# Delta-rule blocks: the convolution's tail three hook steps later, the decay matrices in a chain of their own, one head ahead

## The chip, the cores and the metric

The kernel runs on one core of a Trainium2 chip, as one program of some 40,000 instructions. The metric is the device time of one execution in microseconds (us); lower is better. A core has these engines, each with a queue that it works off in order: PE (TensorE, matmuls and transposes; its weight loads are shown as PEld), DVE (VectorE), ACT (ScalarE), POOL (GpSimd) and SP (SyncE, which here issues every DMA). They meet through semaphores only.

## The reference, cut to what matters

One decoder layer: RMS norm, one wide input projection, two token mixers (a gated delta rule, "DN", and dilated window attention), gates, an output projection, a residual. The change touches the DN inputs. Per head (four heads of width 128, sequence 2048, chunks of 64):

```python
h = rms_norm(x, norm_w); proj = h @ w_in
qkv = silu(causal_depthwise_conv(dn_qkv, conv_w))       # width 4
dq, dk = l2_normalize(dq) * HEAD_DIM ** -0.5, l2_normalize(dk)
gc    = cumsum(g)                                       # log decay, per head and position
decay = exp(where(causal, gc[:, None] - gc[None, :], -inf))
lower   = where(strict, (k * beta) @ k.T * decay, 0)    # inverted later: I + lower
a_intra = where(causal, q @ k.T * decay, 0)
```

## The kernel before

All matmul inputs are float32 split in two float32r parts, so a dense product is three matmuls. The normalised input lies on chip as `hh` and `hl`, in four blocks of 512 positions. The program has stages; the one that matters is `cunits`, which makes 128 projected channels at a time:

- A *unit* is 128 channels; it has four *blocks* (`n` = 0 to 3), one for each 512 positions. A block is 24 dense matmuls (L400 to L402) into a PSUM tile `mm` (three buffers), with one call of `hook()` after every six: four *hook steps* a block. Then the unit's function is called with the block's PSUM tile.
- The units in order: three `z` units, then for each head a k unit, a q unit and a v unit (`k_block`, `q_block`, `v_block`), then the other `z` units and sixteen `g` units. Under the later ones run the inverse of the 64x64 triangles (DVE) and the scan over chunks.
- `self.at(d, fn)` puts `fn` on a list; it is called d hook steps later. So hooks set the order in which instructions are *written down*. The order in each engine's queue is made after that, when the program is built, by a list scheduler with a plan of its own: of the instructions whose inputs and buffers are ready in its plan it takes the one written down first. An instruction written late can so stand early in a queue.

What the three block functions do:

- `conv` (all three): ACT copies the PSUM tile to `xr` (L500) and makes a first product `acc` (L503); DVE adds three shifted products (L505); ACT takes a tanh (L507) and DVE ends the SiLU (L508) into `kT` or `qT`.
- `k_block`: `kT` goes to DRAM (`recput`, L511). A DMA fetches the cumulated log decay, spread over all partitions, to `gcb` (L523, one buffer); DVE adds the mask (L526) and combines (L530, four); ACT takes four exponentials (L532) into the decay matrix `E`. `E` is one tile of 16 matrices, for a whole head. Eight and nine hook steps later, `pe(0)` and `pe(2)` transpose two 128x128 parts of `kT` each (L539) to a PSUM tile `tp` (two buffers), which ACT reads (L543, L544), and POOL makes norms in seven small steps (L552 to L558).
- `q_block`: k and q are split again for the products of k with k and q: ACT copies (`kqh`, L574 and L576), POOL subtracts for k (L575) and DVE for q (L577) into `kql`. `kqh`, `kql` and `la` have one buffer. `pe(0)` and `pe(2)`, again 8 and 9 hook steps later, do for each of two parts one transpose (L585) and three matmuls into the PSUM tile `sc` (L586 to L588, where L587 needs both halves of `kql`); ACT squares the transposed parts (L590), DVE multiplies by `E` into `la` (L591); after the second one `la` goes out by four DMAs and POOL makes norms in three steps (L603 to L605).
- `v_block`: four transposes (L618), 8 hook steps after the block, and ACT scales them (L621).

Of the kernel before, what the change touches and what calls it, by code (L numbers as in the profile page):

```python
# [6 lines left out]
F32 = mybir.dt.float32  # L7
# [34 lines left out]
class Net:  # L42
# [449 lines left out]
    def conv(self, n, ct, pr, dst):  # L492
        nc, dp = self.nc, self.dp
        xr = dp.tile([P, 515], F32, name="xr", bufs=2)
        if n == 0:
            nc.gpsimd.memset(xr[:, 0:3], 0.0)
        else:
            nc.vector.tensor_copy(xr[:, 0:3], self.xr[:, 512:515])
        self.xr = xr
        nc.scalar.activation(xr[:, 3:515], pr, AF.Copy)  # L500
        acc = dp.tile([P, 512], F32, name="acc", bufs=2)
        w = self.cw[:, ct, :]
        nc.scalar.activation(acc, pr, AF.Identity, scale=w[:, 3:4])  # L503
        for j in (2, 1, 0):
            nc.vector.scalar_tensor_tensor(out=acc, in0=xr[:, j:j + 512], scalar=w[:, j:j + 1], in1=acc,  # L505
                                           op0=ALU.mult, op1=ALU.add)
        nc.scalar.activation(dst, acc, AF.Tanh, scale=0.5)  # L507
        nc.vector.scalar_tensor_tensor(out=dst, in0=dst, scalar=1.0, in1=acc, op0=ALU.add, op1=ALU.mult)  # L508
# [4 lines left out]

    def k_block(self, h, n, pr):
        nc, dp = self.nc, self.dp
        if n == 0:
            self.kT = dp.tile([P, T], F32, name="kT", bufs=1)
            self.E = dp.tile([P, 16, P], F32, name="E", bufs=1)
        kT, E = self.kT[:, n * 512:(n + 1) * 512], self.E
        self.conv(n, 4 + h, pr, kT)  # L520
        self.recput(n, h, R_KT, P, kT.rearrange("p (a c) -> p a c", c=P))
        gcb = dp.tile([P, 2, 4, P], F32, name="gcb", bufs=1)
        nc.sync.dma_start(gcb.rearrange("p a b c -> p a (b c)"),  # L523
                          dr(self.gcscr, h * T + n * 512, [[0, P], [H * T, 2], [1, 512]]))
        En = E[:, n * 4:n * 4 + 4, :]
        nc.vector.tensor_tensor(out=gcb[:, 1], in0=gcb[:, 1], in1=self.cmask.unsqueeze(1).to_broadcast([P, 4, P]),  # L526
                                op=ALU.add)
        for t in range(4):
            c = h * 16 + n * 4 + t
            nc.vector.scalar_tensor_tensor(out=gcb[:, 0, t], in0=gcb[:, 0, t], scalar=self.ngc[:, c:c + 1],  # L530
                                           in1=gcb[:, 1, t], op0=ALU.add, op1=ALU.add)
            nc.scalar.activation(En[:, t, :], gcb[:, 0, t], AF.Exp, bias=self.nlc[:, c:c + 1])  # L532
        ss = dp.tile([P, 12], F32, name="ss", bufs=2)
        kd = dp.tile([P, 4, P], F32, name="st4", bufs=2)

# [23 lines left out]
        self.at(8, lambda: pe(0))  # L559
        self.at(9, lambda: pe(2))  # L560

    def q_block(self, h, n, pr):
        nc, dp = self.nc, self.dp
        qT = dp.tile([P, 512], F32, name="qT", bufs=2)
        self.conv(n, h, pr, qT)
        self.recput(n, h, R_QT, P, qT.rearrange("p (a c) -> p a c", c=P))
        kT, E = self.kT, self.E
# [6 lines left out]
        nc.scalar.activation(kqh[:, :, 0, :], kv, AF.Copy)  # L574
        nc.gpsimd.tensor_tensor(out=kql[:, :, 0, :], in0=kv, in1=kqh[:, :, 0, :].bitcast(F32), op=ALU.subtract)  # L575
        nc.scalar.activation(kqh[:, :, 1, :], qv, AF.Copy)  # L576
        nc.vector.tensor_tensor(out=kql[:, :, 1, :], in0=qv, in1=kqh[:, :, 1, :].bitcast(F32), op=ALU.subtract)  # L577

        def pe(t0):
            pt = self.ps.tile([P, 512], F32, name="tp", bufs=2)  # L580
            pk = self.ps.tile([P, 512], F32, name="sc", bufs=2)
            for t in (t0, t0 + 1):
                b = pk[:, (t - t0) * 256:(t - t0) * 256 + 256]
                rh, rl = (a[:, t].rearrange("p a c -> p (a c)") for a in (kqh, kql))
                nc.tensor.transpose(pt[:, (t - t0) * P:(t - t0 + 1) * P], qT[:, t * P:(t + 1) * P], self.ident)  # L585
                nc.tensor.matmul(b, kqh[:, t, 0, :], rh, start=True, stop=False)  # L586
                nc.tensor.matmul(b, kqh[:, t, 0, :], rl, start=False, stop=False)  # L587
                nc.tensor.matmul(b, kql[:, t, 0, :], rh, start=False, stop=True)  # L588
            for t in (t0, t0 + 1):
                nc.scalar.activation(sq, pt[:, (t - t0) * P:(t - t0 + 1) * P], AF.Square, accum_out=ss[:, t:t + 1])  # L590
            nc.vector.tensor_tensor(out=la[:, t0:t0 + 2], in0=pk.rearrange("p (a b c) -> p a b c", b=2, c=P),  # L591
                                    in1=E[:, n * 4 + t0:n * 4 + t0 + 2, :].unsqueeze(2).to_broadcast([P, 2, 2, P]),
# [13 lines left out]
        self.at(8, lambda: pe(0))  # L606
        self.at(9, lambda: pe(2))

    def v_block(self, h, n, pr):
        nc, dp = self.nc, self.dp  # L610
        vT = dp.tile([P, 512], F32, name="qT", bufs=2)
        self.conv(n, 8 + h, pr, vT)
# [10 lines left out]
        self.at(8, pe)  # L623
# [280 lines left out]
    def run(self):  # L904
# [69 lines left out]
        self.cunits(first + du + rest, {3: open_dn, 15: lambda: self.at(9, start_inverse)}, tail)  # L974
# [61 lines left out]
```

## Time and profile before

| | |
|---|---|
| time, three runs | 2415.37, 2414.56, 2415.00 us; median 2415.0 us |
| span of the profiled execution | 2415.5 us (first to last instruction, the only time that it has of its own; 0.5 us over the median) |
| busy: PE, PEld, DVE, ACT, POOL | 2360.4, 2144.5, 1165.6, 848.5, 825.0 us |
| mean granted clock of PE | 0.996 |
| k, q and v units of the four heads | 1126.9 to 1463.5 us of the span |
| a unit with nothing else on PE (z4, from 1486.6 us) | 21.98 us |
| k, q and v unit of head 1 | 25.47, 30.05 and 28.57 us |

A line of the profile gives the source line, the engine, the operation, the tiles (out<-in), the busy time and the mean duration of one, and what the engine waited for before it. PE's busy time counts a matmul to its modelled end, so 98% is no proof of full speed; how close matmuls start behind one another tells more. The clock column is the share of full TensorE speed that was granted. What an engine waited for is inferred from semaphores.

### The profile page before, as it was taken

The page shows a single profiled execution, that of the slowest core. Times are in us where ns is not written, and L with a number is a line of the kernel's source. Part 1 is how long each engine was busy: PE and PEld are TensorE (multiplying, and loading weights), DVE is VectorE, ACT ScalarE, POOL GpSimd, SP SyncE. Part 2 cuts the span into 40 slices and gives each one's busy share as a digit, 9 for nine tenths or more (in the row PEclk, how much of TensorE's full clock was granted, in tenths as well). Part 3 has the DMA queues.
Part 4 walks back from the last instruction along what each step waited for, and adds up shares of the span by engine and source line. Part 5 has one row for each costly group of instructions (what it writes and reads, how often), then busy time and mean ns, then how long its engine had stood idle before and what let it go on. Part 6 is the DMA issues. An engine that isn't in the chain of part 4 may idle for free.

```text
span 2415.5 us, 40131 instructions
## 1 busy us (share of the span) xinstructions
PE 2360.4 (98%) x13710; PEld 2144.5 (89%) x13710; DVE 1165.6 (48%) x2738; ACT 848.5 (35%) x2985; POOL 825.0 (34%) x1785
## 2 busy tenths in 40 slices
PE   7999999999999999999999999999999999999999
PEld 7999999999999999987777778888888878889998
DVE  5644333233343433344766665999444433454431
ACT  5644433334443333323665663111243313111110
POOL 4433334433333334411433451111133212433441
PEclk9999999999999999999999999999999999999999
DMA  5211102333433343433544443222566655555442
GB/s 157 73 48 39 28 25 64 94 92 102 114 106 92 112 118 89 115 98 102 129 120 111 116 119 113 75 75 73 180 198 195 185 162 158 162 180 161 146 139 76
DMA packets 348819, 274.22 MB, mean 114 GB/s; under 512 B 57864, under 2 KB 317256, under 8 KB 348232
## 3 DMA queue, kind: packets, MB, share of 16 engines
q1 hardware_dynamic: 348616, 271.66, 39.1%
q8 instruction: 109, 1.79, 0.3%
q14 instruction: 94, 0.77, 0.1%
HBM read 167.47 MB, written 104.10 MB: 112 GB/s over the span
## 4 chain that ended last, share of the span: by engine, by line
PE 83%; DMA 7%; DVE 3%; ACT 3%; issue 2%; POOL 2%; SPq 1%; ACTq 0%; DVEq 0%; POOLq 0%
PE mm L167 10%; PE mm L169 10%; PE mm L168 10%; PE mm L400 8%; PE mm L402 8%; PE mm L401 8%; DMA gcb<-gcscr 3%; PE mm L888 2%; PE mm L886 2%; PE mm L887 2%; PE mm L869 2%; PE mm L871 2%; PE mm L870 2%; PE po L265 2%; PE tp L222 2%
## 5 line engine op out<-in xcount | busy, mean ns | idle before, releaser
L167 PE MATMUL mm<-wh,hh 128*128 128x384 f32 (+1 forms) x1536 | 553.5, 360 | 3.8 <-ACT wh L79 3.8
L169 PE MATMUL mm<-wh,hl 128*128 128x384 f32 (+1 forms) x1536 | 519.3, 338 | 0.0
L168 PE MATMUL mm<-wl,hh 128*128 128x384 f32 (+1 forms) x1536 | 518.6, 338 | 0.1
L400 PE MATMUL mm<-hh,wh 128*128 128x512 f32 x1152 | 467.2, 406 | 0.0
L402 PE MATMUL mm<-hh,wl 128*128 128x512 f32 x1152 | 454.9, 395 | 0.0
L401 PE MATMUL mm<-hl,wh 128*128 128x512 f32 x1152 | 453.5, 394 | 0.0
L167 PEld LDWEIGHTS mm<-wh,hh 128*128 128x128 f32 x1536 | 289.9, 189 | 6.6 <-ACT wh L79 4.2
L168 PEld LDWEIGHTS mm<-wl,hh 128*128 128x128 f32 x1536 | 290.7, 189 | 0.4 <-POOL wl L80 0.4
L169 PEld LDWEIGHTS mm<-wh,hl 128*128 128x128 f32 x1536 | 289.2, 188 | 0.0
L402 PEld LDWEIGHTS mm<-hh,wl 128*128 128x128 f32 x1152 | 217.6, 189 | 47.6
L400 PEld LDWEIGHTS mm<-hh,wh 128*128 128x128 f32 x1152 | 218.1, 189 | 44.5
L401 PEld LDWEIGHTS mm<-hl,wh 128*128 128x128 f32 x1152 | 218.2, 189 | 41.2
L80 POOL TENSOR_TENSOR wl<-raw,wh 128x512 fp32r<-128x512 f32 (+1 forms) x75 | 108.1, 1453 | 397.6 <-ACT wh L79 397.5
L190 DVE SCALAR_TENSOR_TENSOR rec<-mm,st,wqk 128x128 f32<-128x128 f32 x256 | 78.1, 347 | 264.1 <-POOL st L188 233.6
L186 POOL TENSOR_SCALAR st<-st 128x2 f32<-128x2 f32 x192 | 44.9, 234 | 419.8 <-ACT rec L182 284.5
L249 ACT ACTIVATE p<-sc,ol 128x128 f32<-128x128 f32 (+1 forms) x192 | 82.1, 427 | 299.3 <-DVE ol L247 287.3
L869 PE MATMUL mm<-oh,hh 128*128 128x256 f32 x512 | 143.8, 281 | 1.9 <-DVE gt L873 1.9
L505 DVE SCALAR_TENSOR_TENSOR acc<-xr,cw,acc 128x512 f32<-128x512 f32 x144 | 122.6, 851 | 44.1 <-ACT acc L503 40.7
L871 PE MATMUL mm<-oh,hl 128*128 128x256 f32 x512 | 142.9, 279 | 0.0
L870 PE MATMUL mm<-ol,hh 128*128 128x256 f32 x512 | 142.9, 279 | 0.0
L188 POOL TENSOR_TENSOR st<-st,mhalf 128x2 f32<-128x2 f32 x192 | 135.1, 704 | 16.0
L79 ACT ACTIVATE wh<-raw 128x512 fp32r<-128x512 f32 (+1 forms) x145 | 90.0, 632 | 110.8 <-PE mm L401 73.4
(240 smaller groups left out, 4320.4 us busy)
## 6 DMA issues: line engine op xcount, KB each, us to landing
raw<-in_w_in_dram SPq DMA_DIRECT2D x144, 256.0 KB, 3.3
rscr<-rec SPq DMA_DIRECT2D x128, 192.0 KB, 1.9
qk<-rscr SPq DMA_DIRECT2D x128, 128.0 KB, 2.3
gscr<-gt SPq DMA_DIRECT2D x64, 256.0 KB, 2.5
gt<-gscr SPq DMA_DIRECT2D x64, 256.0 KB, 3.5
oscr<-ol SPq DMA_DIRECT2D x192, 65.0 KB, 1.9
oc<-oscr SPq DMA_DIRECT2D x16, 780.0 KB, 5.0
rec<-rec SPq DMA_DIRECT2D x16, 768.0 KB, 5.6
```

Of the source, the lines that this page charges most:

```text
L80: eng.tensor_tensor(out=l, in0=raw, in1=h.bitcast(F32), op=ALU.subtract)
L167: nc.tensor.matmul(pr[:, :w], a, wh[:, k, :w], start=(k == 0), stop=False)
L168: nc.tensor.matmul(pr[:, :w], a, wl[:, k, :w], start=False, stop=False)
L169: nc.tensor.matmul(pr[:, :w], b, wh[:, k, :w], start=False, stop=(k == KT - 1))
L188: nc.gpsimd.tensor_tensor(out=st[:, 2:4], in0=st[:, 0:2], in1=self.mhalf[:, 0:2], op=ALU.pow)
L400: nc.tensor.matmul(pr, wh[:, k, :], a, start=(k == 0), stop=False)
L401: nc.tensor.matmul(pr, wh[:, k, :], b, start=False, stop=False)
L402: nc.tensor.matmul(pr, wl[:, k, :], a, start=False, stop=(k == KT - 1))
L505: nc.vector.scalar_tensor_tensor(out=acc, in0=xr[:, j:j + 512], scalar=w[:, j:j + 1], in1=acc, op0=ALU.mult, op1=ALU.add)
L869: nc.tensor.matmul(o, self.wbh[:, k, ms], oh[:, k, :], start=(k == b * 4), stop=False)
L870: nc.tensor.matmul(o, self.wbh[:, k, ms], ol[:, k, :], start=False, stop=False)
L871: nc.tensor.matmul(o, self.wbl[:, k, ms], oh[:, k, :], start=False, stop=(k == b * 4 + 3))
```

## The change

- `conv` writes down its last two steps (tanh L507 and the SiLU's end L508), and all that follows on them, three hook steps later, in a function `gate`. The transposes then come six and seven hook steps after that: 9 and 10 after the block in k and q, 8 as before in v.
- The decay matrices leave `k_block`. A function `e_chain` fetches `gcb`, adds the mask on POOL (not DVE) four hook steps later, and combines and exponentiates one step after that. `E` is now a tile for each block, with four buffers. The chain of head 0 is started when the DN memory is opened, a block every 6 hook steps; that of head h+1 after the first v block of head h, a block every 8 hook steps, so it is spread over the v unit of one head and the k unit of the next.
- In `q_block` both subtractions into `kql` are on POOL (the one for q was on DVE), and `pe` writes its two transposes ahead of its six matmuls instead of one ahead of each three.
- The inverse starts 12 hook steps into the unit behind the last v unit, not 9.
- Some comments are gone.

```diff
-    def conv(self, n, ct, pr, dst):
+    def conv(self, n, ct, pr, dst, then):
...
-        nc.scalar.activation(dst, acc, AF.Tanh, scale=0.5)
-        nc.vector.scalar_tensor_tensor(out=dst, in0=dst, scalar=1.0, in1=acc, op0=ALU.add, op1=ALU.mult)
+        def gate():
+            nc.scalar.activation(dst, acc, AF.Tanh, scale=0.5)
+            nc.vector.scalar_tensor_tensor(out=dst, in0=dst, scalar=1.0, in1=acc, op0=ALU.add, op1=ALU.mult)
+            then()
+        self.at(3, gate)
...
+    def e_chain(self, h, period, n=0):
+        if h == H:
+            return
+        nc, dp = self.nc, self.dp
+        gcb = dp.tile([P, 2, 4, P], F32, name="gcb", bufs=1)
+        nc.sync.dma_start(gcb.rearrange("p a b c -> p a (b c)"),
+                          dr(self.gcscr, h * T + n * 512, [[0, P], [H * T, 2], [1, 512]]))
+        def low():
+            nc.gpsimd.tensor_tensor(out=gcb[:, 1], in0=gcb[:, 1],
+                                    in1=self.cmask.unsqueeze(1).to_broadcast([P, 4, P]), op=ALU.add)
+        def high():
+            E = self.E[h, n] = dp.tile([P, 4, P], F32, name="E", bufs=4)
+            for t in range(4):
+                c = h * 16 + n * 4 + t
+                nc.vector.scalar_tensor_tensor(out=gcb[:, 0, t], in0=gcb[:, 0, t], scalar=self.ngc[:, c:c + 1],
+                                               in1=gcb[:, 1, t], op0=ALU.add, op1=ALU.add)
+            for t in range(4):
+                c = h * 16 + n * 4 + t
+                nc.scalar.activation(E[:, t, :], gcb[:, 0, t], AF.Exp, bias=self.nlc[:, c:c + 1])
+        self.at(4, low)
+        self.at(5, high)
+        if n + 1 < NB:
+            self.at(period, lambda: self.e_chain(h, period, n + 1))
...
     def k_block(self, h, n, pr):
...
-            self.E = dp.tile([P, 16, P], F32, name="E", bufs=1)
...
+        def then():
+            self.recput(n, h, R_KT, P, kT.rearrange("p (a c) -> p a c", c=P))
+            self.at(6, lambda: pe(0))
+            self.at(7, lambda: pe(2))
...
-        self.at(8, lambda: pe(0))
-        self.at(9, lambda: pe(2))
+        self.conv(n, 4 + h, pr, kT, then)
...
     def q_block(self, h, n, pr):
...
-        nc.scalar.activation(kqh[:, :, 0, :], kv, AF.Copy)
-        nc.gpsimd.tensor_tensor(out=kql[:, :, 0, :], in0=kv, in1=kqh[:, :, 0, :].bitcast(F32), op=ALU.subtract)
-        nc.scalar.activation(kqh[:, :, 1, :], qv, AF.Copy)
-        nc.vector.tensor_tensor(out=kql[:, :, 1, :], in0=qv, in1=kqh[:, :, 1, :].bitcast(F32), op=ALU.subtract)
+        def then():
+            self.recput(n, h, R_QT, P, qT.rearrange("p (a c) -> p a c", c=P))
+            for j, src in enumerate((kv, qv)):
+                nc.scalar.activation(kqh[:, :, j, :], src, AF.Copy)
+                nc.gpsimd.tensor_tensor(out=kql[:, :, j, :], in0=src, in1=kqh[:, :, j, :].bitcast(F32),
+                                        op=ALU.subtract)
+            self.at(6, lambda: pe(0))
+            self.at(7, lambda: pe(2))
...
             for t in (t0, t0 + 1):
+                nc.tensor.transpose(pt[:, (t - t0) * P:(t - t0 + 1) * P], qT[:, t * P:(t + 1) * P], self.ident)
+            for t in (t0, t0 + 1):
...
-                nc.tensor.transpose(pt[:, (t - t0) * P:(t - t0 + 1) * P], qT[:, t * P:(t + 1) * P], self.ident)
...
     def v_block(self, h, n, pr):
...
-        self.at(8, pe)
+        self.conv(n, 8 + h, pr, vT, lambda: self.at(5, pe))
+        if n == 0:
+            self.e_chain(h + 1, 8)
...
             self.dp = pool(dst, "dp", "right")
+            self.E = {}
+            self.e_chain(0, 6)
...
-        self.cunits(first + du + rest, {3: open_dn, 15: lambda: self.at(9, start_inverse)}, tail)
+        self.cunits(first + du + rest, {3: open_dn, 15: lambda: self.at(12, start_inverse)}, tail)
```

More of the change, by code (lines that the diff above doesn't have):

```diff
@@ L517, in k_block @@
             self.kT = dp.tile([P, T], F32, name="kT", bufs=1)
-            self.E = dp.tile([P, 16, P], F32, name="E", bufs=1)
[L519 to L532, printed above, removed]
+        kT = self.kT[:, n * 512:(n + 1) * 512]
         ss = dp.tile([P, 12], F32, name="ss", bufs=2)
         kd = dp.tile([P, 4, P], F32, name="st4", bufs=2)
+        def then():
+            self.recput(n, h, R_KT, P, kT.rearrange("p (a c) -> p a c", c=P))
+            self.at(6, lambda: pe(0))
+            self.at(7, lambda: pe(2))
         def pe(t0):
@@ L564, in q_block @@
         qT = dp.tile([P, 512], F32, name="qT", bufs=2)
-        self.conv(n, h, pr, qT)
-        self.recput(n, h, R_QT, P, qT.rearrange("p (a c) -> p a c", c=P))
-        kT, E = self.kT, self.E
+        kT = self.kT
         ss = dp.tile([P, 12], F32, name="ss", bufs=2)
@@ L605, in pe @@
                 G.tensor_scalar(out=self.cq[:, cs], in0=ss[:, 4:8], scalar1=SCALE, scalar2=None, op0=ALU.mult)
-        self.at(8, lambda: pe(0))
-        self.at(9, lambda: pe(2))
+        self.conv(n, h, pr, qT, then)
     def v_block(self, h, n, pr):
@@ L611, in v_block @@
         vT = dp.tile([P, 512], F32, name="qT", bufs=2)
-        self.conv(n, 8 + h, pr, vT)
         vs = dp.tile([P, 4, P], F32, name="st4", bufs=2)
```

2 lines of the change are left out of this document (1 added, 1 removed).

## The prediction, as it was put on record before the changed kernel had run

> **What bounds the kernel now.** I read the page first, then the busy times of the DN units, then PE's waits there, then the order of time around the longest.
>
> ```profile
> PE 2360.4 (98%) x13710; PEld 2144.5 (89%) x13710; DVE 1165.6 (48%) x2738; ACT 848.5 (35%) x2985; POOL 825.0 (34%) x1785
> PE 83%; DMA 7%; DVE 3%; ACT 3%; issue 2%; POOL 2%; SPq 1%; ACTq 0%; DVEq 0%; POOLq 0%
> ```
>
> PE carries the kernel, and the change removes no PE work, so all it can win is time in which PE stands still. The windows of head 1's k, q and v units, of head 2's q unit and of a bare unit (us, then busy time of PE, PEld, DVE, ACT, POOL, granted clock, DMA), and of single blocks, give how much that is:
>
> ```profile
> 1213.97:1239.44 25.47, 23.82 (x114) 19.26 (x112) 15.96 (x30) 15.30 (x45) 4.23 (x3) 1.00 0.48 114
> 1239.44:1269.49 30.05, 27.89 (x132) 22.72 (x132) 19.14 (x32) 20.36 (x71) 19.84 (x37) 0.94 0.47 126
> 1269.49:1298.06 28.57, 28.06 (x147) 23.32 (x145) 18.98 (x28) 15.65 (x49) 10.69 (x14) 1.00 0.50 108
> 1323.83:1353.85 30.02, 27.88 (x133) 22.68 (x133) 19.56 (x32) 20.36 (x71) 19.81 (x37) 0.94 0.47 127
> ...
> 1262.09:1269.49 7.40, 7.40 (x42) 6.30 (x41) 4.80 (x8) 4.33 (x14) 4.78 (x10) 1.00 0.45 119
> 1298.06:1304.00 5.94, 5.94 (x31) 4.90 (x30) 4.17 (x8) 4.41 (x12) 2.88 (x2) 1.00 0.30 78
> 1486.56:1492.05 5.49, 5.49 (x25) 4.51 (x24) 2.29 (x2) 1.61 (x3) 2.58 (x2) 1.00 0.67 217
> ```
>
> A bare block takes 5.49 us, one with four transposes 5.94, one with a q block's sixteen extra PE instructions 7.40. A head without stalls is then 12 x 5.49 + 8 x 0.45 + 4 x 1.91 = 77.1 us; head 1 takes 25.47 + 30.05 + 28.57 = 84.1. So some 7 us a head, under 30 us in all, could be won. PE's own waits (waited for, us, times, longest), over all DN units and then without those of head 0's k and q, and DVE's largest DMA wait, say where:
>
> ```profile
> PE tp L539 <- ACT st L544: 11.9, 7, 2.2
> ...
> PE tp L539 <- ACT st L544: 9.8, 5, 2.2
> PE sc L587 <- DVE kql L577: 1.6, 4, 0.5
> PE sc L587 <- POOL kql L575: 0.6, 1, 0.6
> ...
> DVE gcb L526 <- DMA gcb<-gcscr: 25.1, 16, 3.4
> ```
>
> The k transposes wait for ACT to empty `tp`. Why ACT is late is in the order of time (start, us, engine, line, idle before and its releaser):
>
> ```profile
> 1241.99 0.69 DVE L508 SCALAR_TENSOR_TENSOR kT<-kT,acc 128x512 f32<-128x512 f32 x1 [0.70 <-ACT kT L507]
> 1246.08 1.21 DVE L526 TENSOR_TENSOR gcb<-gcb,cmask 128x512 f32<-128x512 f32 x1 [3.40 <-DMA gcb<-gcscr]
> 1250.48 0.63 ACT L507 ACTIVATE kT<-acc 128x512 f32<-128x512 f32 x1 [4.21 <-DVE acc L505]
> 1253.53 0.66 PE L539 MATMUL tp<-ident,kT 128*128 128x128 f32 x2 [2.16 <-ACT st L544]
> 1254.41 0.63 PE L401 MATMUL mm<-hl,wh 128*128 128x512 f32 x1
> ```
>
> DVE stands 3.40 us before the mask for a DMA that has not landed; the convolution behind it in DVE's queue is late, so ACT stands 4.21 us before the tanh, so `tp` is emptied late, so PE stands 2.16 us, and then a dense matmul takes 0.63 us. That q unit has a granted clock of 0.94, as has head 2's. The chain is thus: DMA of `gcb`, DVE, ACT, PE, clock. Who wrote this load so early is the next view, of SP and ACT:
>
> ```profile
> 1168.97 0.36 SPq L523 DMA_DIRECT2D gcb<-gcscr  x1
> 1240.57 0.36 SPq L523 DMA_DIRECT2D gcb<-gcscr  x1
> 1288.88 1.28 ACT L532 ACTIVATE E<-gcb,nlc 128x128 f32<-128x128 f32 x4
> 1291.28 0.55 SPq L523 DMA_DIRECT2D gcb<-gcscr  x1
> ```
>
> The load of 1240.57 is head 2's first, 57 us ahead of head 2's k unit (1298.06); 1168.97 is head 1's first. The planner already hoists it; its exponentials run at 1288.88, when the last `la` of head 1 has let the one `E` tile go. After that the chain loads again, in time for the k unit to suffer.
>
> **The change, part by part.**
>
> *`E` in four buffers, a chain of its own.* The number of loads, combinations and exponentials stays 16, 64 and 64. What moves is when: block n of the next head may be exponentiated as soon as the q unit has used block n of this one, so I expect the loads to run through the q and v units, not to bunch in k. In k, DVE then has only the convolution. I take the five waits of heads 1 to 3 as gone: -9.8 us; bounds 0 (the waits stay, below) and -11.9 (head 0's go too; I keep these 2.1 us, since its chain has to start as early as now and finds the same engines). With them goes the slow clock: (1 - 0.94) x 30.05 = 1.8 us in each of two units, -3.6 us; bounds 0 and -3.6. What is late next in k: nothing that I see; ACT is busy 15.3 of 25.5 us and DVE 16.0.
>
> *The tail three steps later.* Per block one ACT and one DVE instruction, the `recput` DMA on SP and in q four more (two on ACT, two subtractions). A step is 5.49 / 4 = 1.37 us, so the transposes are asked for 1.4 us later in k and q and at the same step in v; no other stage waits for a single block. On ACT, the reads of `tp` are now written ahead of the tanh, which helps the same waits that I have counted. On SP, the block's `recput` is passed by what is written in those three steps, a weight load at most, which serves the next unit and has most of a unit's time. I take 0, bounds -2.2 (the L587 waits of heads 1 to 3) and +1.4 for each unit of 12 where a step is not hidden (+16.8, far).
>
> *Mask on POOL.* 16 instructions of 0.69 us leave DVE; on POOL each takes what the k subtraction takes there, 1.43 (rows below). DVE's time is not what PE waits for once it does not stand for the DMA: 0, with the case that POOL stands instead as a rival.
>
> *Both subtractions on POOL.* This one costs. The rows of one turn, from the second PE part of a q block (n = 2) to the first of the next:
>
> ```profile
> L575 POOL TENSOR_TENSOR kql<-kT,kqh x16: 1310/1432/1600, 1146.5 to 1448.2; 128x512 fp32r<-128x512 f32 x16
> L577 DVE TENSOR_TENSOR kql<-qT,kqh x16: 680/692/1694, 1174.3 to 1447.4; 128x512 fp32r<-128x512 f32 x16
> ...
> 1278.96 0.27 PE L585 MATMUL tp<-ident,qT 128*128 128x128 f32 x1
> 1279.43 0.27 PE L585 MATMUL tp<-ident,qT 128*128 128x128 f32 x1
> 1280.47 0.62 ACT L574 ACTIVATE kqh<-kT 128x512 fp32r<-128x512 f32 x1
> 1280.65 0.23 POOL L603 TENSOR_SCALAR ss<-ss 128x4 f32<-128x4 f32 x1 [4.55 <-ACT sq L590]
> 1282.09 0.66 POOL L605 TENSOR_SCALAR cq<-ss 128x4 f32<-128x4 f32 x1
> 1282.83 1.59 POOL L575 TENSOR_TENSOR kql<-kT,kqh 128x512 fp32r<-128x512 f32 x1
> 1284.03 0.27 PE L585 MATMUL tp<-ident,qT 128*128 128x128 f32 x1
> 1284.48 0.38 PE L587 MATMUL sc<-kql,kqh 128*128 128x256 f32 x1
> ```
>
> `kqh` and `kql` have one buffer, so the turn is closed: PE's second part, squares, POOL's norms (1280.65 to 1282.75), k's subtraction (to 1284.42), L587 at 1284.48. There is no slack left in it (L587 would start 0.2 us behind the transpose, 1284.26, and comes 0.2 later). The second subtraction behind it adds 1.43 + 0.08. Against that, the two transposes ahead of the matmuls start the squares 0.36 us earlier (the second transpose comes 0.45 / 4 = 0.11 instead of 0.47 behind the first), and L587 0.11 later: 1.51 - 0.36 - 0.11 = 1.04, so PE waits 1.25 in place of 0.2. Where no wait is left over now (n = 1) I take 0.8, an estimate from the same row with 0.2 us of slack; where the wait now is for DVE's stretched 1.69 us (0.46 us, which goes) a net 0.5. So 0.8 + 0.5 + 0.85 = 2.15 us a head, the 0.85 for the last turn with a POOL run of 1.43, not 1.59: +8.6 us. Bounds 0 (POOL takes k's subtraction ahead of the norms) and 12 x 1.51 = +18.1. I take 8.6, by the row of this very loop. Each such wait stays under the 2.16 us after which the clock fell.
>
> *Transposes together, fewer names.* The number of PE instructions is the same: 0.
>
> *Inverse three steps later.*
>
> ```profile
> 1490.45 7.53 DVE L641 TENSOR_TENSOR M<-Z,nb 128x4096 f32<-128x4096 f32 x1 [2.08 <-DMA Z<-lscr]
> 1497.89 0.67 DVE L785 SCALAR_TENSOR_TENSOR gt<-gt,mm 128x512 f32<-128x512 f32 x1
> ```
>
> All behind it moves by 4.1 us, and nothing waits for its end but the last stage, which takes its order from hooks too. What queues behind L641 on DVE is the gate of the block that ended at 1492.05; it holds one of three `mm` buffers, which PE wants again at 1492.05 + 2 x 5.49 = 1503.0. It is free at 1498.6 now and at 1502.7 then: covered by 0.3 us, cost 0, bounds 0 and +4.1 if the cover is gone.
>
> **The sum.** Against the span of 2415.5: -9.8 - 3.6 + 8.6 = -4.8, so 2410.7; the median of the runs is 0.5 lower. I say 2411 us, a gain that is just what a measurement of this kernel can tell from none (0.2%, 4.8 us). Its own range is 2405 to 2416: from the head-0 waits and half of the subtraction's cost less, to the k waits half kept.
>
> **The rivals.**
>
> *POOL stands for the DMA (slower).* The mask waits for `gcb` wherever it lies. If the planner puts it in POOL's queue between a q block's subtractions and the next norms, the norms wait for the landing. By the rows above, the chain goes on when `la` is done: at head 1's end the second PE part starts at 1286.67, the next load is issued at 1291.28, 4.6 us later; the tile's row says when it lands.
>
> ```profile
> DMA to landing us min/median/max: 4.7/5.2/5.9
> ```
>
> So the mask ends 4.6 + 5.2 + 1.43 = 11.2 us behind that start. The next norms are ready 7.4 + 0.85 (PE's new wait) + 1.33 (1280.65 - 1278.96 - 0.36) = 9.6 behind it: 1.6 us late, 2.3 for the slowest load. Two turns a head in three heads (the last has no next) give 6 x 1.6 = 9.6 us. Then PE's waits are 2.5 to 3, over 2.16, and the clock falls 1.8 us in perhaps half of them, 5.4: 2411 + 15 = 2426 us. It decides from 0.75 us a turn on (6 x 0.75 = 4.5 us, all of the gain). For it speaks that DVE stood up to 3.4 us for this DMA, since the planner had it landed sooner; against it, that POOL is also given the next unit's weights there and that a load finished one turn later hurts nobody. The Trainium skill (TensorE: Matmul & The Clock Gate, Why this matters for your kernels) says that gaps up to about 3 us leave the clock at full speed. By that rule this rival would be 5.4 us cheaper, 2421. The trace disagrees with it here: 2.16 us were enough, so the sum goes by the row.
>
> *The subtraction is hidden.* If POOL takes k's subtraction when ACT has copied k (1281.1), ahead of the longest norm step, both are done about 1.4 us sooner and L587 waits no more than now: 2411 - 8.6, and up to 2.2 less with the waits that are there now, about 2401. For it: the subtraction is written ahead of the norms. Against: it is so in the kernel before too, and POOL took all three norm steps first.
>
> *The change does not do what it says.* The load was a head ahead before. If DVE stands for POOL where it stood for the DMA, the k waits stay, half of 13.4 us: 2411 + 6.7 = 2418.
>
> **Chances.** Forecast 0.45, half of it over 0.2% faster and half within; hidden subtraction 0.14, all faster; change without effect 0.13, of that 0.10 within and 0.03 slower; POOL stands 0.28, 0.03 of it within. That gives faster 0.37, within 0.2% 0.35, slower 0.28. The range leaves out the best of the second case and the worst of POOL's (a fall of the clock in each turn, 2431): 2398 to 2427. As both signs hold much, the forecast's own range above stands beside it.
>
> **What would show it.** Right: no wait of L539 for ACT in heads 1 to 3, k units near 4 x 5.94 = 23.8 us, a clock of 1.00 in all q units, a second L575 in the turn and L587 waiting 0.8 to 1.3 us for POOL in twelve turns, `gcb` loads spread over q and v. Wrong: a POOL idle time before the mask, ended by the DMA, with norms behind it, and q units over 31 us; or L539 still waiting.

## The result and the profile after

The changed kernel takes 2433.4 us (median of four runs, 2432.2 to 2434.7); the kernel before, run beside it, 2415.2. The ratio is 1.0067 with a 95% interval of 1.0055 to 1.0080: 18 us slower by the medians and 16 by the ratio, where 2411 was forecast. The profiled execution has a span of 2430.4 us, 14.9 over that of before. Of all runs below one was slow, 2890 us in e3 beside 2409 to 2416 for its others, and e3's ratio goes without it.

Two stages hold nearly all of it. From the first dense matmul of k0 to that of z4 it was 359.7 us and is 372.0 (+12.4); from z4 to g13, where the scan ends, 482.6 and 484.1 (+1.5); the stages ahead of k0 are 1.0 longer. The windows from k0 to z4 before and after, then of the changed kernel head 0 whole and the k, q and v unit of head 1 (columns: us, busy time of PE, PEld, DVE, ACT, POOL, granted clock, DMA):

```profile
1126.90:1486.56 359.66, 341.71 (x1657) 278.77 (x1656) 226.04 (x378) 211.34 (x665) 141.25 (x214) 0.99 0.47 118
...
1127.87:1499.89 372.02, 345.30 (x1657) 281.62 (x1656) 218.29 (x346) 211.05 (x665) 182.11 (x246) 0.98 0.44 112
...
1127.87:1226.16 98.29, 84.59 (x400) 67.60 (x399) 53.68 (x107) 52.62 (x173) 46.47 (x65) 0.97 0.47 118
1226.16:1250.49 24.33, 23.67 (x111) 19.19 (x110) 16.37 (x24) 12.42 (x31) 5.43 (x5) 1.00 0.34 93
1250.49:1276.24 25.75, 25.43 (x125) 20.77 (x124) 17.74 (x25) 20.28 (x73) 19.59 (x34) 1.00 0.43 119
1276.24:1311.42 35.18, 30.79 (x153) 25.54 (x152) 19.77 (x33) 18.88 (x61) 20.83 (x23) 0.95 0.53 127
```

From k0 to z4 PE stands still for 26.7 us where it was 18.0 (the length less PE's busy time). The clock is halved there in four stretches of 3.41 us each, where it was in two, and such a stretch costs half its length, 1.7 us. The two together are 8.8 + 3.4 = 12.2 of the 12.4 us.

In head 1 the k unit has gone from 25.47 to 24.33 us and the q unit from 30.05 to 25.75 with its clock back at 1.00: what was forecast of the chain came. The v unit went from 28.57 to 35.18, with 153 PE instructions instead of 147 (a later tail moves some transposes there, 0.1 us each). So head 1 as a whole is 1.2 us longer, head 2 0.9 longer and head 3 0.9 shorter: what k and q win, v loses. Head 0 wins nothing and takes 98.3 us for 87.1. PE's and then POOL's waits over the DN units say what they stand for (us in total, times, longest; in the new line numbers the mask is L528, the split copies and subtractions are L597 and L598, and L612 is the matmul that needs both halves of `kql`, L587 before; the last row is of the kernel before):

```profile
PE sc L612 <- POOL kql L598: 15.8, 8, 3.6
PE tp L561 <- ACT st L566: 5.8, 5, 3.2
...
POOL gcb L528 <- DMA gcb<-gcscr: 34.3, 7, 12.8
...
PE sc L587 <- POOL kql L575: 2.3, 2, 1.7
```

The 11.9 us of waits for the transposes (L539 before, L561 now) are down to 5.8, most of it in head 0; the waits for `kql` are up from 3.9 (2.3 for POOL, 1.6 for DVE) to 15.8. Here is the longest, in v1 (POOL's and PE's order of time: start, us, what it did):

```profile
1281.59 1.75 POOL L80 TENSOR_TENSOR wl<-raw,wh 128x512 fp32r<-128x512 f32 x1
1283.32 0.66 POOL L628 TENSOR_SCALAR ss<-ss 128x4 f32<-128x4 f32 x1
...
1285.51 1.26 POOL L528 TENSOR_TENSOR gcb<-gcb,cmask 128x512 f32<-128x512 f32 x1
1286.73 1.26 POOL L598 TENSOR_TENSOR kql<-kT,kqh 128x512 fp32r<-128x512 f32 x1
1287.95 1.31 POOL L598 TENSOR_TENSOR kql<-qT,kqh 128x512 fp32r<-128x512 f32 x1
...
1289.31 0.54 PE L612 MATMUL sc<-kql,kqh 128*128 128x256 f32 x1 [3.58 <-POOL kql L598]
1290.51 0.63 PE L400 MATMUL mm<-hh,wh 128*128 128x512 f32 x1
```

POOL works without a gap: a weight split, the norms (L628 to L630), the mask, both subtractions. It does not stand for a DMA here. PE waits 3.58 us for the last, and the dense matmul behind it takes 0.63 us, the slow clock. In head 0, where 23.0 of POOL's 34.3 us of waits for the load lie, the mask stands for its load, DVE stands for the mask, ACT for DVE, and PE for ACT:

```profile
1171.49 1.27 POOL L528 TENSOR_TENSOR gcb<-gcb,cmask 128x512 f32<-128x512 f32 x1 [0.88 <-DMA gcb<-gcscr]
1172.79 0.35 DVE L535 SCALAR_TENSOR_TENSOR gcb<-gcb,ngc 128x128 f32<-128x128 f32 x1 [4.81 <-POOL gcb L528]
1173.17 0.40 ACT L539 ACTIVATE E<-gcb,nlc 128x128 f32<-128x128 f32 x1 [4.86 <-DVE gcb L535]
...
1175.09 0.44 PE L561 MATMUL tp<-ident,kT 128*128 128x128 f32 x2 [3.21 <-ACT st L566]
```

### The profile page after: what moved, and what is told of

It reads as the page before. It is cut to its first block, busy times and chain, and to the rows that moved or that the text cites. A ratio compares the mean times of both kernels' runs of the same rounds, so it can differ in the third digit from the quotient of the medians.

```text
span 2430.4 us, 40167 instructions
## 1 busy us (share of the span) xinstructions
PE 2365.0 (97%) x13710; PEld 2149.8 (88%) x13710; DVE 1155.2 (48%) x2706; ACT 848.0 (35%) x2985; POOL 866.1 (36%) x1817
## 5 line engine op out<-in xcount | busy, mean ns | idle before, releaser
L80 POOL TENSOR_TENSOR wl<-raw,wh 128x512 fp32r<-128x512 f32 (+1 forms) x75 | 113.6, 1530 | 379.0 <-ACT wh L79 378.6
L505 DVE SCALAR_TENSOR_TENSOR acc<-xr,cw,acc 128x512 f32<-128x512 f32 x144 | 116.0, 806 | 47.2 <-ACT acc L503 44.2
```

The source lines that it names most:

```text
L80: eng.tensor_tensor(out=l, in0=raw, in1=h.bitcast(F32), op=ALU.subtract)
```

## The experiments

The table has every run: median, ratio to the kernel before on the same chip with its interval, and the stretch from k0 to z4 in the profiled execution (359.7 before, 372.0 after).

| run | what it is | us | ratio | k0 to z4 |
|---|---|---|---|---|
| e1 | after, mask on DVE | 2418.0 | 1.000 (0.999 to 1.001) | 360.4 |
| e2 | after, q subtraction on DVE | 2426.0 | 1.0033 (1.0020 to 1.0046) | 367.7 |
| e3 | after, both on DVE | 2413.6 | 0.9979 (0.9969 to 0.9989) | 351.7 |
| e4 | after, tail at once | 2431.6 | 1.0050 (1.0033 to 1.0067) | 371.9 |
| e5 | after, masks held back | 2433.6 | 1.0069 (1.0055 to 1.0083) | 375.4 |
| e6 | e3, masks held back | 2410.2 | 0.9974 (0.9962 to 0.9985) | 348.4 |
| e7 | e3, tail at once: the chain alone | 2404.6 | 0.9946 (0.9934 to 0.9959) | 344.3 |
| e8 | e3, inverse at 9 | 2410.3 | 0.9972 (0.9961 to 0.9982) | 352.6 |
| e9 | before, tail alone | 2408.6 | 0.9960 (0.9944 to 0.9976) | 350.0 |
| e10 | e7, inverse at 9 | 2402.0 | 0.9932 (0.9917 to 0.9946) | 343.4 |
| e11 | e7, q subtraction on POOL | 2423.8 | 1.0025 (1.0013 to 1.0037) | 362.5 |
| e12 | e7, mask on POOL | 2422.3 | 1.0021 (1.0011 to 1.0031) | 362.1 |
| e13 | e3, weight split on DVE | 2407.7 | 0.9960 (0.9946 to 0.9975) | 341.6 |
| e14 | e10, transposes one by one | 2405.7 | 0.9956 (0.9944 to 0.9969) | 350.0 |
| e15 | before, q subtraction on POOL | 2431.8 | 1.0068 (1.0048 to 1.0088) | 371.6 |
| e16 | e3, inverse at 9, DN weight split on DVE | 2403.6 | 0.9955 (0.9941 to 0.9968) | 343.9 |
| e17 | e10, DN weight split on DVE | 2400.1 | 0.9934 (0.9921 to 0.9946) | 341.6 |

### The two moves to POOL, undone one at a time

e1:
```diff
-            nc.gpsimd.tensor_tensor(out=gcb[:, 1], in0=gcb[:, 1],
+            nc.vector.tensor_tensor(out=gcb[:, 1], in0=gcb[:, 1],
```


> After the change, with the mask (L528) back on DVE and all else as it is. Theory P, POOL's string: between two q blocks POOL does the norms, the mask and both subtractions in series, and the matmul L612 waits for the last of them; in head 0 POOL also stands for the mask's DMA. Without the mask heads 1 and 2 lose 1.3 of the 3.58 us stall, the 0.81 us stall and about 1.6 us of halved clock each (some 3.7 us a head), and head 0 loses most of its L612 stalls and their clock (4.5 + 3): 2417 to 2423 us. Theory L, late tail: what is late is the tanh and the SiLU's end, three hook steps after the block, so that any engine would be late; only the mask's own 1.3 us per turn can go: 2428 to 2432. Theory D, the DMA of head 0's matrices: the wait goes from POOL to DVE and costs PE the same there; heads 1 and 2 gain, head 0 does not: 2425 to 2428.

e2 (e3 has both edits):
```diff
-                nc.gpsimd.tensor_tensor(out=kql[:, :, j, :], in0=src, ...
+                (nc.gpsimd, nc.vector)[j].tensor_tensor(out=kql[:, :, j, :], in0=src, ...
```


> After the change, with the subtraction for q back on DVE (the second of the two L598), the mask still on POOL. Theory P: the string on POOL is one subtraction (1.3 us) shorter, in all heads; the stalls of v1 and v2 fall from 3.58 to about 2.3 us and from 0.81 to 0, that of v3 from 2.46 to 1.2 us with its clock; head 0 keeps the waits for the DMA: 2421 to 2426 us. Theory L: DVE ends no earlier than POOL, since both start from the late tail: 2430 to 2434. Theory D says nothing against P for heads 1 to 3 and keeps head 0's 11 us: 2423 to 2427.

> After the change, with the mask and the subtraction for q both back on DVE; the chain a head ahead, the tail three hook steps later, the transposes together and the later inverse stay. Theory P: this is the change without its two moves to POOL, so heads 1 to 3 lose all of the L612 stalls and most of head 0's: 2408 to 2414 us, no slower than before the change (2415.2). Theory L: 2426 to 2432. Theory D: head 0 keeps most of its 11 us: 2417 to 2421.

All three came out as theory P had it: the mask back on DVE gives back 15 us by the medians (16 by the ratios, which set each run against the kernel before beside it), the subtraction 7 (8), both 20 (21), and with both back the change is a small gain (0.9979). Theory L, that the late tail makes any engine late, is out as the main cause. For e2 alone theory D's range fits as well.

### The tail at once, with the work left on POOL

```diff
-        self.at(3, gate)
+        gate()
...
-            self.at(6, lambda: pe(0))
-            self.at(7, lambda: pe(2))
+            self.at(8, lambda: pe(0))
+            self.at(9, lambda: pe(2))
```
(and `at(8, pe)` for `at(5, pe)` in v.)

> After the change, with the convolution's tail written down at once as before (transposes 8 and 9 hook steps after the block in k and q, 8 in v); mask and both subtractions stay on POOL. Theory P: the string on POOL is as long as it was and cannot start before the matmuls of the block before have read kqh and kql, so the stalls stay: 2429 to 2436 us. Theory L: the stalls of v1, v2, v3 and of head 0 go with the delay: 2414 to 2420. Theory D: head 0 unchanged, within 2 us of after in all.

2431.6, and 371.9 us from k0 to z4 against 372.0: as P had it. While POOL sets the turns, the tail's place is worth next to nothing.

### The mask held back out of the turns

```diff
-        self.conv(n, 8 + h, pr, vT, lambda: self.at(5, pe))
+        self.conv(n, 8 + h, pr, vT, lambda: (n == 1 and nc.vector.tensor_scalar(out=self.cmask[:, P - 1:P],
+                  in0=vT[:, 0:1], scalar1=0.0, scalar2=None, op0=ALU.mult), self.at(5, pe)))
```
(The hold is a dependency, since an instruction that is only written down later can still stand early in a queue.)

> After the change, mask and both subtractions on POOL as there; one small DVE instruction a head writes zeros over a column of the mask that is zero already, from the v unit's second finished block, so that no mask of the next head can be added before the closed turns of q (both in the first two blocks of the v unit) are over. It adds work and takes none away. Theory P (it is the mask's place in the queue, between the norms and the subtractions): v1 and v2 fall from 35.2 us to what v3 takes, which has no chain behind it (31.4), v0 by about as much: 2433.4 - 7.6 - 3.8 = 2422, range 2419 to 2425. Rival (the amount of work on POOL, wherever it stands): 2431 to 2435. Second rival (the matrices then come late for the next head's q): q units of heads 1 to 3 grow from 25.7 us by more than 2 us each: 2428 or more.

> The kernel with mask and q subtraction on DVE, with the same hold. There the mask stood on DVE in front of the subtraction for q (1.78 us at 1277.44, beside POOL's subtraction). Theory P: v1 and v2 (32.3 and 30.8 us) fall to v3's 29.6, v0 (34.4) to about 31.5: 2413.6 - 7 = 2406 to 2410, ratio to the kernel before about 0.9955. Rival (the turn is set by the copies, subtractions and norms themselves, the mask is beside them): 2412 to 2415. Second rival (late matrices): over 2414.

e5 did what P said to the v units (v1 35.2 to 32.4, v2 35.2 to 30.8) and won nothing: 2433.6, as both rivals had it. The matrices' work ran on into the next k and q units, and the waits moved with it: q1 and q2 are 4.9 us longer, not for want of matrices but for the k transposes behind ACT (3.3 us in q1, and 1.7 us of halved clock). PE's waits in e5, and the q and v unit of head 1:

```profile
PE tp L561 <- ACT st L566: 13.0, 9, 2.4
PE sc L612 <- POOL kql L598: 10.3, 5, 3.1
...
1247.53:1278.17 30.64, 27.30 (x125) 21.88 (x124) 20.01 (x31) 23.82 (x81) 22.07 (x36) 0.94 0.37 105
1278.17:1310.56 32.39, 30.33 (x154) 25.30 (x152) 18.32 (x29) 15.77 (x50) 18.39 (x20) 0.95 0.48 107
```

So theory P, as the place of the mask between norms and subtractions, was only half of it. With the mask on DVE the same hold (e6) came to the upper edge of what P gave, 2410.2, with 30.2 us for v1 and v2; the intervals of e3 and e6 overlap.

### The good part by itself, and each move added to it

e7 is e3 with the edit of e4: the chain, `E` in four buffers, the transposes together and the later inverse.

> The kernel before with the chain and E in four buffers, the transposes together and the inverse three steps later, but with the convolution's tail at once, the mask and the q subtraction on DVE: all of the change but its tail and its moves to POOL. Theory C (the chain alone frees the k units; the later tail frees the q units of the L561 kind of wait and moves q's products into v): k about 23.7, q about 27.4, v about 29 to 30 us in heads 1 to 3, so 1.5 to 2.5 us a head more than with the later tail: 2416 to 2421. Rival (the later tail is worth nothing): 2411 to 2415, the same as with it.

2404.6, better than either guess: the rival's range lay too high, and theory C's sign was wrong, since the later tail is a cost beside the chain. PE's waits over all DN units, and the k, q and v unit of head 1:

```profile
PE tp L561 <- ACT st L566: 2.1, 1, 2.1
...
PE sc L612 <- POOL kql L598: 0.2, 1, 0.2
...
1216.59:1240.33 23.74, 23.74 (x114) 19.25 (x112) 15.06 (x24) 13.10 (x37) 4.17 (x4) 1.00 0.35 100
1240.33:1266.64 26.31, 26.27 (x132) 21.70 (x132) 17.75 (x26) 21.07 (x74) 21.51 (x37) 1.00 0.45 122
1266.64:1294.57 27.93, 27.93 (x147) 23.28 (x145) 22.92 (x41) 16.82 (x54) 11.88 (x13) 1.00 0.61 151
```

The head takes 23.74 + 26.31 + 27.93 = 78.0 us, where 77.1 was worked out for one without a stall. Of the waits for `tp`, one is left, in head 0. To this kernel e11 adds the q subtraction on POOL (the edit of e2 left out), e12 the mask on POOL (the edit of e1 left out):

> The chain alone, with the subtraction for q on POOL (mask on DVE, tail at once). Theory P (POOL's string): in the closed turn POOL has norms and two subtractions of 1.3 to 1.7 us in series where DVE took one of them; L612 waits 0.5 to 1.5 us in two or three turns a head: 2409 to 2415. Rival (a tail at once leaves room for it; only the mask hurts): 2404 to 2406.

> The chain alone, with the mask on POOL (q subtraction on DVE, tail at once). With both on POOL and the tail at once it was 2431.6, without either 2404.6: 27 us to share out. Theory D (POOL stands for the matrices' DMA with the subtraction for k and the norms behind it, and ACT and DVE follow): most of it, 2416 to 2426, with the worst of it in head 0 (its units took 97.9 us with both on POOL, 87.7 without either). Rival (the two moves only hurt together, by the length of the string): 2406 to 2412.

Each costs 18 to 19 us by itself, but the two together only 27 (e4, 2431.6). Theory D had the mask's price right but not its place, since heads 0, 1 and 2 take 5.5 to 5.8 us each; theory P had the subtraction far too low. D's order of things is in a row of DVE's waits for e7, and one of DVE's and three of PE's for e12:

```profile
DVE gcb L528 <- DMA gcb<-gcscr: 12.2, 12, 1.9
```

```profile
DVE gcb L535 <- POOL gcb L528: 37.7, 16, 3.4
...
PE tp L561 <- ACT st L566: 6.7, 4, 4.4
PE sc L612 <- POOL kql L598: 6.7, 4, 1.9
PE tp L641 <- DVE qT L510: 4.3, 2, 2.4
```

With the mask on DVE, DVE waits 12.2 us in all for the loads. With the mask on POOL it waits 37.7 us, every time, for another engine that waits for the load and then takes 1.3 us where DVE takes 0.7. ACT's waits for DVE's combination go from 14.3 us to 48.3. Of PE's waits, those for POOL's `kql` are up by 6.5 us on e7; those behind ACT and DVE by 9.9 (L561 2.1 in e7, L641 none, and 1.0 for one L611 behind the tanh). In k1 of e12 it goes on as it did in the kernel before (`qT` is in the profile also the name of the v unit's tile):

```profile
1229.38 1.30 POOL L528 TENSOR_TENSOR gcb<-gcb,cmask 128x512 f32<-128x512 f32 x1 [0.68 <-DMA gcb<-gcscr]
1230.71 2.17 DVE L535 SCALAR_TENSOR_TENSOR gcb<-gcb,ngc 128x128 f32<-128x128 f32 x4 [3.19 <-POOL gcb L528]
1235.15 0.63 ACT L509 ACTIVATE qT<-acc 128x512 f32<-128x512 f32 x1 [5.21 <-DVE acc L505]
...
1236.56 0.66 PE L641 MATMUL tp<-ident,qT 128*128 128x128 f32 x4 [2.38 <-DVE qT L510]
```

That is the chain of the prediction's first part with one more engine in it, and here with the v transposes at its end: DMA, POOL, DVE, ACT, DVE, PE.

### The q subtraction on POOL, on the kernel before

```diff
-        nc.vector.tensor_tensor(out=kql[:, :, 1, :], in0=qv, ...
+        nc.gpsimd.tensor_tensor(out=kql[:, :, 1, :], in0=qv, ...
```


> The kernel before with the subtraction for q on POOL and nothing else changed: the term that the sum put at 8.6 us (both subtractions in series on POOL; waits of 0.8, 0.5 and 0.85 us a turn). If that term was right: 2422 to 2426 against 2415 to 2418 for the kernel before. If POOL's string costs what it cost beside the chain (19 us: 2423.8 against 2404.6): 2433 to 2437. If the cost comes only where the chain's masks and exponentials run in the v unit: 2416 to 2420.

2431.8 against 2417.1: 14.7 us, between the term of the sum (8.6) and what it cost beside the chain. PE's wait for it over all DN units:

```profile
PE sc L587 <- POOL kql L577: 17.2, 12, 3.5
```

Twelve waits in twelve turns were forecast, of 0.8 to 1.3 us; they came, six of 0.7 to 0.9 us and six of 1.4 to 3.5, 13.3 us more in all than in the kernel before (3.9), where the sum had 8.6. The k transposes wait 3.9 us less here (8.0 for 11.9), and the clock is halved for two more stretches (3.4 us), both behind the longest wait.

### Why the later tail and the chain lose together

e9 makes `conv` of the kernel before write its tail and what follows three steps later, with the calls of e4's diff the other way round; nothing else.

> The kernel before with the convolution's tail alone three hook steps later (transposes 9 and 10 steps after the block in k and q, 8 in v); the decay matrices stay in the k blocks, the mask and the q subtraction on DVE, the inverse at 9. Theory T (the later tail lands in the closed turn of q: tanh on ACT and the SiLU's end on DVE come after the last matmul of one block and stand ahead of the next block's copies and subtractions): L612's counterpart waits 1 to 2 us in the turns that fall into the v unit, with halved clock behind it, as in the kernel with mask and q subtraction on DVE (v units 29.6 to 32.3 us), so 1 to 3 us a head more: 2419 to 2427 us. Rival (the later tail only costs where a chain of matrices runs in the v unit): 2413 to 2418.

2408.6: alone, the later tail gains 9.6 us, on which neither theory had bet. It frees the k units (25.5 to 23.45 us) as the chain does, by another way; q1 and q2 stay at 29.8 and 30.6. Together (e3) they gain 3.5. The turn of v1 in e3 (order of time of POOL, DVE, ACT and PE) shows what meets:

```profile
1271.29 3.03 POOL L80 TENSOR_TENSOR wl<-raw,wh 128x512 fp32r<-128x512 f32 x2
1271.30 3.57 DVE L505 SCALAR_TENSOR_TENSOR acc<-xr,cw,acc 128x512 f32<-128x512 f32 x2 [1.62 <-ACT acc L503]
1276.16 0.63 ACT L509 ACTIVATE qT<-acc 128x512 f32<-128x512 f32 x1 [2.57 <-DVE acc L505]
1276.70 0.61 ACT L597 ACTIVATE kqh<-kT 128x512 fp32r<-128x512 f32 x1
1277.44 1.78 DVE L528 TENSOR_TENSOR gcb<-gcb,cmask 128x512 f32<-128x512 f32 x1
1279.14 0.68 DVE L598 TENSOR_TENSOR kql<-qT,kqh 128x512 fp32r<-128x512 f32 x1
1279.97 0.36 PE L612 MATMUL sc<-kql,kqh 128*128 128x256 f32 x1 [1.70 <-DVE kql L598]
```

Two of the three L505 take 3.57 us beside POOL's L80 (1.5 would be usual). ACT stands 2.57 us for them before the next block's tanh, and behind that tanh are the copies of the block whose turn it is, which could have gone at 1273.4, when L613 was done. e13 takes L80 off POOL:

```diff
-            self.split(raw, wh[:, k:k + 4, :], wl[:, k:k + 4, :], nc.gpsimd)
+            self.split(raw, wh[:, k:k + 4, :], wl[:, k:k + 4, :], nc.vector)
```


> The kernel with mask and q subtraction on DVE (tail three steps later, 2413.6), with the low part of the weights (L80) made on DVE, not POOL. In the trace of that kernel two L80 on POOL in the v unit stretch DVE's L505 beside them from 0.74 to 1.85 and 1.68 us, and ACT's queue has the next block's tanh (L509, 2.57 us waited for L505) ahead of the copies kqh of the block whose turn it is (L597). Here L505 is not stretched there and the tanh stands behind the copies. Theory A (the tanh ahead of the copies is what the later tail costs together with the chain): the stalls of v1 and v2 (1.8 and 1.85 us, with clock) go, 32.3 and 30.8 us become about 29: 2406 to 2410. Rival (the mask on DVE ahead of the subtraction makes the stall, whatever ACT does): 2412 to 2416. Second rival (DVE has eight more subtractions of 0.7 us a unit and becomes late itself): over 2416.

The same turn in e13:

```profile
1266.04 0.74 DVE L505 SCALAR_TENSOR_TENSOR acc<-xr,cw,acc 128x512 f32<-128x512 f32 x1
1267.49 0.64 ACT L597 ACTIVATE kqh<-kT 128x512 fp32r<-128x512 f32 x1
1268.55 0.61 ACT L509 ACTIVATE qT<-acc 128x512 f32<-128x512 f32 x1
...
1270.15 1.34 DVE L528 TENSOR_TENSOR gcb<-gcb,cmask 128x512 f32<-128x512 f32 x1 [1.51 <-DMA gcb<-gcscr]
1271.42 0.68 DVE L598 TENSOR_TENSOR kql<-qT,kqh 128x512 fp32r<-128x512 f32 x1
1272.24 0.35 PE L612 MATMUL sc<-kql,kqh 128*128 128x256 f32 x1 [0.38 <-DVE kql L598]
```

The copies are ahead of the tanh, the mask still stands ahead of the subtraction on DVE, and the stall is 0.38 us, not 1.70: theory A, and not the mask. (The edit ends the stretch of L505 and turns the order of tanh and copies on ACT; no run parts the two.) v1 and v2 take 29.15 and 29.14 us. The edit also slowed the scan's stage (487.1 us from z4 to g13, 483.7 in e3), so e16 and e17 keep it to the DN units, with the inverse at 9:

```diff
+ ..., nc.vector if C_DN <= c < C_DN + 1536 else nc.gpsimd)
```


> Tail three steps later, chain, mask and q subtraction on DVE, inverse at 9, and the low part of the weights (L80) on DVE for the k, q and v units alone, on POOL elsewhere. With the weight split on DVE everywhere the stretch from k0 to z4 took 341.6 us (343.4 for the chain alone with the inverse at 9), and that from z4 to g13 487.1 (482.5 there), where the split stood among the inverse on DVE. Theory A (with the stretch of L505 gone the later tail costs nothing beside the chain): 2403 - 5 = 2398 to 2403, as fast as the chain alone or faster. Rival: the later tail keeps costs of its own, 2405 to 2409.

> The chain alone (tail at once) with the inverse at 9 and the same weight split on DVE in the k, q and v units. Theory A: here the copies stood ahead of the tanh already and PE waited for almost nothing in heads 1 to 3, so there is little to gain: 2399 to 2403. Rival (POOL beside DVE stretches other steps too, in head 0 above all, where L561 waits 2.7 us): 2394 to 2399. Second rival (DVE's extra work comes in the way): 2403 or more.

With the later tail 2403.6 and without it 2400.1: of the 9 us between e3 and e7, 3.5 are left, and the intervals overlap. Theory A holds for most of it, as far as the medians tell. The remainder is in v units 1.3 to 1.6 us longer in heads 1 to 3 (29.2, 29.2 and 29.6 against 27.9, 27.8 and 28.0), for which no run was made; head 0 differs the other way.

### The parts that were put at nothing

e8 and e10 put the inverse back:
```diff
-        ... {3: open_dn, 15: lambda: self.at(12, start_inverse)}, tail)
+        ... {3: open_dn, 15: lambda: self.at(9, start_inverse)}, tail)
```


> The kernel with mask and q subtraction on DVE, with the inverse started 9 hook steps in as before, not 12. The stage of the scan's end has one stall: 5.2 us at g12 with the later inverse (L878 behind DVE's L863), 3.6 us at g11 in the kernel before, each with halved clock behind it. If that step costs what the two traces show: 1 to 2 us less, 2411.5 to 2413. If the end of the scan only falls elsewhere: within 1 us of 2413.6.

> The chain alone (tail at once, mask and q subtraction on DVE, transposes together), with the inverse at 9 as before. From the traces of the two places of the inverse, the stretch from z4 to g13 is 483.7 against 481.6 us: 2 us less, 2402 to 2403.5. If the end of the scan depends on the stages ahead of it more than on this step: 2404 to 2406.

Both came 2.6 to 3.3 us lower and the stretch from z4 to g13 shorter by 2.1 and 0.7 (481.6 for 483.7, 482.5 for 483.2). PE's longest wait there is 5.3 us in the changed kernel and 3.9 in e10 (L878, for DVE's L863). The intervals overlap, so a cost of 1 to 3 us is likely and not shown. e14 undoes the order of the transposes in e10, one ahead of each three matmuls:

> The chain alone with the inverse at 9 (2402.0), with the q transposes one ahead of each three matmuls as before, not two ahead of six. If the order of the transposes is worth nothing, as it was put in the sum: 2401 to 2403. If two transposes ahead give ACT its input earlier, so that the squares and the PSUM buffer come free earlier: 2404 to 2407 without it.

2405.7 against 2402.0, and 350.0 against 343.4 us from k0 to z4: the transposes together are worth 4 to 7 us (the two intervals just overlap). PE's waits in heads 1 to 3 of e14 (whose L611 is the other kernels' L612), where e10 has one of 0.2 us:

```profile
PE tp L561 <- ACT st L566: 1.8, 2, 1.2
PE sc L611 <- DVE kql L598: 1.1, 3, 0.4
PE sc L611 <- POOL kql L598: 1.0, 2, 0.5
```

e10 and e17 are the fastest versions: 0.9932 and 0.9934 of the kernel before, some 16 us less.

## Why the prediction was wrong, by its own steps

From before to after on one path of measured kernels, each against the kernel before beside it: the chain with the transposes and the inverse (e7) -11.9 us; the later tail on top (e3) -3.5, so +8.4; the q subtraction on POOL on top (e1) +0.9, so +4.4; the mask on POOL on top (after) +18.2, so +17.3. By the ratios the four kernels stand at -13, -5, 0 and +16. The order of the path matters: on e7 the subtraction is worth +19, the mask +18, both +27 (e4), and the later tail on top of both 2 us by the medians, 4 by the ratios.

- *The chain: right.* -13.4 was put on the L539 waits and their clock; -11.9 was measured with two smaller parts in it, and the k units came to 23.7, 23.6 and 23.6 us in heads 1 to 3 of e7 (23.8 forecast). Head 0's wait stayed, as said.
- *The mask on POOL: the step that failed.* It was put at 0, since DVE's time is not what PE waits for, with a rival for the case that POOL stands for the load. It costs 17 to 18 us on e1 and on e7, and 8 where the subtraction is on POOL already (e11 to e4). The rival came nearest, at 15 us and 2426, and had POOL stand for the load; but by it the q units were to take over 31 us, and in heads 1 to 3 they take 25.5 to 25.8. In v1 and v2 the mask stands for nothing and adds its 1.3 us to a full string. The rival sized only what stands behind the mask on POOL. The larger part in e12 is what waits for the mask: DVE's 37.7 us, and behind DVE the convolution (9.9 us of PE's added waits, 6.5 behind POOL).
- *The tail: failed too.* 0, with its ends at -2.2 and +16.8 by step. It is -9.6 alone and +8.4 beside the chain. The step argued from what is written ahead of the tanh; with the chain the tanh stands ahead of the next copies. The step did not have that ACT waits there for DVE's L505, slowed by POOL.
- *Both subtractions on POOL: mis-sized.* 8.6 in the sum, 14.7 measured alone, inside its bounds of 0 to 18.1, and 19 beside the chain, outside them. The twelve waits came, six of them longer than the row of one turn had it, and behind the longest (3.5 us, in head 0) the clock fell.
- *Transposes together: mis-sized.* Put at 0 because the instructions are as many; worth 4 to 7 us, of waits for `kql` and for `tp` that come back without it. The step had seen 0.36 and 0.11 us of a turn, and had used them in the subtraction's term alone.
- *The inverse:* 0 with a bound of +4.1; 1 to 3 us, not settled.
- *The clock:* waits "under the 2.16 us after which the clock fell" were taken as safe. In the changed kernel it fell behind waits of 1.67 and 2.01 us in v0; what decides is not the length of one wait (last section).

## What to carry to other kernels

In this kernel work that waits for a DMA belongs on the engine that uses the result, although that engine is the busier one: a helper in between adds its own queue, its own duration and a second hand-over, and all that queues behind the user's wait is late. POOL, with 36% busy time, had no slack inside a turn that is closed by single buffers, so cost a move there by the length of that string. Two edits that each remove the same stall are to be tried apart before they are put together.

## What the runs showed of the hardware

POOL's two-input operations stretch DVE's here: L505 takes 0.74 us alone, and two took 3.57 beside L80 in the turn of e3; with L80 on DVE (e13) they take 0.74 in that turn. The Trainium skill (SBUF — State Buffer, SBUF: two separate sides) says that DVE and GpSimd share a port pair as an exclusive lock and that the other one blocks; the two rows agree.

The clock does not fall at one length of gap. In the changed kernel 3.21 us (q0) and 2.46 us (v3) left it alone, and 1.67 us (v0) did not. The granted clock shows why. Between the start and the end of every trace it falls to a half for 3.41 us, or for twice that, and all its changes lie whole multiples of 3.41 us apart: it is set window by window, on a grid that runs on through the program. What counts is how long PE stands still within one window, all its gaps together. Two windows of the changed kernel, each with the one behind it (the first busy time is PE's, the third figure from the end the clock):

```profile
1173.33:1176.74 3.41, 1.65 (x8) 1.27 (x9) 2.58 (x6) 3.38 (x17) 0.47 (x2) 1.00 0.01 2
1176.74:1180.16 3.42, 3.42 (x17) 2.87 (x17) 1.77 (x3) 3.09 (x10) 3.00 (x7) 1.00 0.47 121
...
1190.40:1193.81 3.41, 1.59 (x10) 1.14 (x9) 0.09 (x1) 3.41 (x11) 3.33 (x4) 1.00 0.82 187
1193.81:1197.22 3.41, 3.41 (x13) 2.84 (x12) 3.12 (x4) 1.67 (x10) 3.24 (x4) 0.50 0.94 168
```

The gap of 3.21 us is cut by the grid into 1.76 us and 1.44 in the window before, and the clock stays. That of 1.67 us lies whole in one window, with 0.15 us of smaller gaps it makes 1.82, and the next window has half the clock. Over the first 1900 us of the 19 traces no window at full clock with under 1.68 us of standing is followed by a fall (some 10300 windows), and each with over 1.85 us is (53 windows); of the 38 in between 14 are. So about half a window of standing is the limit, and e11 has a case on each side of it: the same wait of 1.78 us, with 1.75 us of standing in its window in v1 and 1.78 in v2, and a dense matmul of 0.40 us after the first and of 0.63 after the second. The Trainium skill (TensorE: Matmul & The Clock Gate, Part 1: The HAM clock gate) says that activity is watched in a free-running window of some 3.4 us. The traces agree with that window, but half of it idle was enough here, where the page of the Trainium skill asks for a whole one.
